# A matrix product with leaky ReLU: 32-bit transposes of A, and a first unit of k in two half segments

## Chip, cores, metric

One core of a Trainium2 chip. The metric is the device time of one execution in microseconds (us); quoted times are medians of repeated executions. "Spell" below means a stretch in which TensorE runs at half clock: in the trace its weight loads then follow each other every 427 ns and not every 216. In the kernel before, the granted clock is 0.50 from 102.5 to 109.3 us, where such a stretch lies. At the start only the pitch of 427 ns tells: the record of the granted clock begins only at 13.75 us in the trace of before. "Full clock" means the pitch of 216.

## The reference

```python
def setup_inputs():
    m, k, n = 4096, 4096, 4096
    return {"a": np.random.randn(m, k).astype(np.float32),
            "b": np.random.randn(k, n).astype(np.float32),
            "alpha": np.float32(0.01)}

def reference(a, b, alpha):
    x = np.matmul(a, b)
    return np.where(x > 0, x, alpha * x)
```

## The kernel before

The product is made in bf16, in regions of 512 rows by 1024 columns: 4 x 2 tiles of 128x512, each in one of eight PSUM buffers (`banks` in the code). k is cut into units of 1024, that is 8 groups of 128. A comes to SBUF with k along the free axis and is transposed there. In the steady part a piece of A (256 rows, one unit) is fetched by four GpSimd DMAs, which also round it to bf16 (128 KB each as written), and transposed by VectorE; the code lays it out in blocks of 32x32 for this:

```python
KC, NT, MT, NP = 8, 512, 4, 2
TURNS = [[0], [1], [2, 3]]

def new_a(mb, h, u):                    # A transposed, one unit of one half: 512 rows
    at[mb, h, u] = at_pool.tile([P, KC, RM], BF16, name="at")

def load_a(mb, h, u, mp):
    dst = new_a(mb, h, u)[:, :, 2 * mp * P:2 * (mp + 1) * P]
    row = (mb * HALVES + h) * RM + 2 * mp * P
    a16 = a16_pool.tile([P, 8, QW], BF16, name="a16")
    for q in range(4):
        src = a[row:row + 2 * P, u * KW + q * QW:u * KW + (q + 1) * QW]
        nc.gpsimd.dma_start(a16[32 * q:32 * q + 32], src.rearrange("(g i) w -> i g w", i=32))
    nc.vector.transpose(
        dst.rearrange("p c (g i) -> p g c i", g=8), a16.rearrange("p g (j c) -> p g c j", c=KC)
    )

def mm(ps, mb, h, pi, u, mt, nt, c, first, last):
    nc.tensor.matmul(ps, at[mb, h, u][:, c, mt * P:(mt + 1) * P],
                     bt[pi, u][:, c, nt * NT:(nt + 1) * NT], start=first, stop=last)
```

The first two regions (half 0 and half 1 of the first 1024 rows) are computed while the data is still arriving. They share one set of B, and go by "turns" over k: unit 0 for half 0, then for half 1; unit 1 likewise; then units 2 and 3 for half 0, and for half 1. A "step" is one unit for one half. At the end of a turn the banks are emptied ("spilled") into SBUF, and from the second turn on added to what lies there:

```python
# the start: unit 0 of half 0 comes as fp32 by SyncE's DMAs, without GpSimd
order = [("a", 0), ("b", 0), ("a", 1), ("b", 1), ("b", 2), ("a", 2), ("b", 3), ("a", 3),
         ("b", 4), ("b", 5), ("b", 6), ("b", 7)]           # 512 KB each
# ... each is cast to bf16; rows of A are transposed by TensorE against an identity
#     and copied to `at`; what has arrived is multiplied
if (what, i) == ("b", 3):
    nc.gpsimd.tensor_copy(x[:, :1], b0[:, 2, :1])   # marker: GpSimd's loads wait for this

for i in range(1, len(steps)):
    t, h, u, first, last = steps[i]
    following = queue[i + 1] if 2 <= i and i + 1 < len(steps) else []   # the next step's loads
    # ...
    for quarter in range(4):
        # 16 matmuls; in the last step of a turn they finish one row of tiles
        if last:
            spill(t, h, quarter, banks)      # VectorE: two adds
        quarter_of(following, quarter)       # with it the next step's transposes, on VectorE too
```

The order of emission is the order on each engine: with `spill` ahead of `quarter_of`, VectorE adds first and transposes for the next step after that (in the trace two adds from 98.45 us, the transposes behind them from 99.66).

Of the kernel before, what the change touches and what calls it, by code (L numbers as in the profile page):

```python
# [8 lines left out]
P = 128  # L9
BF16 = mybir.dt.bfloat16  # L10
FP32 = mybir.dt.float32
LRELU = mybir.ActivationFunctionType.Lrelu
KC = 8
NT = 512
MT = 4
NP = 2
# [3 lines left out]
TURNS = [[0], [1], [2, 3]]  # L20
# [3 lines left out]
def kernel(  # L24
# [17 lines left out]

    nc = tc.nc
    M, K = a.shape
# [3 lines left out]

    KW = KC * P
    KU = K // KW  # L50
    RM = MT * P
    RN = NP * NT
    QW = KW // 4
    HALVES = 2
    MB = M // (HALVES * RM)
    NB = N // RN
    assert TURNS[0] == [0] and sorted(sum(TURNS, [])) == list(range(KU))
# [27 lines left out]
    def new_a(mb, h, u):  # L85
        if (mb, h, u) not in at:
            at[mb, h, u] = at_pool.tile([P, KC, RM], BF16, name="at")
        return at[mb, h, u]
# [6 lines left out]
    def load_a(mb, h, u, mp):  # L95

        dst = new_a(mb, h, u)[:, :, 2 * mp * P:2 * (mp + 1) * P]
        row = (mb * HALVES + h) * RM + 2 * mp * P
        a16 = a16_pool.tile([P, 8, QW], BF16, name="a16")
        for q in range(4):  # L100
            src = a[row:row + 2 * P, u * KW + q * QW:u * KW + (q + 1) * QW]
            nc.gpsimd.dma_start(a16[32 * q:32 * q + 32], src.rearrange("(g i) w -> i g w", i=32))  # L102
        nc.vector.transpose(  # L103
            dst.rearrange("p c (g i) -> p g c i", g=8), a16.rearrange("p g (j c) -> p g c j", c=KC)
        )

    def b_rows(n, u, c):
        src = b[u * KW:(u + 1) * KW, n * RN:(n + 1) * RN]
        return src.rearrange("(p c) n -> p c n", c=KC)[:, c, :]

    def load_b(pi, n, u, c):

        nc.gpsimd.dma_start(new_b(pi, u)[:, c, :], b_rows(n, u, c))  # L113

    def mm(ps, mb, h, pi, u, mt, nt, c, first, last):
        nc.tensor.matmul(  # L116
            ps,
            at[mb, h, u][:, c, mt * P:(mt + 1) * P],
            bt[pi, u][:, c, nt * NT:(nt + 1) * NT],
            start=first,  # L120
            stop=last,
        )
# [24 lines left out]
    for pi in range(1, len(pairs)):  # L147
        first = next(i for i, r in enumerate(regions) if r[2] == pi)
        for u in range(KU):
            lead = 2 if pi == 1 else KU  # L150
            loads.setdefault(first * KU + u - lead, []).extend(
                lambda pi=pi, u=u, c=c: load_b(pi, pairs[pi], u, c) for c in range(KC)
            )
    for mb in range(1, MB):
        first = next(i for i, r in enumerate(regions) if r[0] == mb)
        for h in range(HALVES):
            for u in range(KU):
                loads.setdefault(first * KU + h * KU + u - 2 * KU + 1, []).extend(
                    lambda mb=mb, h=h, u=u, mp=mp: load_a(mb, h, u, mp) for mp in range(MT // 2)
                )  # L160

    def quarter_of(pieces, quarter):
# [5 lines left out]
        (t, h, u, i == 0, i == len(turn) - 1)  # L168
        for t, turn in enumerate(TURNS)
        for h in range(HALVES)  # L170
        for i, u in enumerate(turn)
    ]

    def step_loads(h, u):
        if h:
            return [lambda mp=mp: load_a(0, 1, u, mp) for mp in range(MT // 2)]
        made = [lambda c=c: load_b(0, pairs[0], u, c) for c in range(KC)]
        made.insert(4, lambda: load_a(0, 0, u, 1))
        made.insert(0, lambda: load_a(0, 0, u, 0))
        return made  # L180

    queue = [step_loads(h, u) for _, h, u, _, _ in steps]
    part = {}

    def spill(t, h, mt, banks):
# [10 lines left out]
        if t == len(TURNS) - 1:  # L196
# [4 lines left out]

    a_in = bt_pool.tile([P, MT, KW], FP32, name="a_in", tag="bt")
    b_in = [part_pool.tile([P, KC // 2, RN], FP32, name="b_in", tag="part") for _ in range(2)]
    a_rounded = at_pool.tile([P, MT, KW], BF16, name="a_rounded", tag="at")
    order = [("a", 0), ("b", 0), ("a", 1), ("b", 1), ("b", 2), ("a", 2), ("b", 3), ("a", 3),
             ("b", 4), ("b", 5), ("b", 6), ("b", 7)]
    for what, i in order:
        if what == "a":
            nc.sync.dma_start(a_in[:, i, :], a[i * P:(i + 1) * P, :KW])  # L209
        else:  # L210
            nc.sync.dma_start(b_in[i // 4][:, i % 4, :], b_rows(pairs[0], 0, i))  # L211
    a0 = new_a(0, 0, 0)
    b0 = new_b(0, 0)
    turned = {
        (mt, i): psum_pool.tile([P, KC // 2, P], BF16, name="turned", tag="ps")
        for mt in range(MT)
        for i in range(2)
    }
    banks = new_banks()

    def take(what, i):
        if what == "b":
            nc.scalar.copy(b0[:, i, :], b_in[i // 4][:, i % 4, :])  # L223
            return
        nc.vector.tensor_copy(a_rounded[:, i, :], a_in[:, i, :])  # L225
        cols = a_rounded[:, i, :].rearrange("m (p c) -> m c p", c=KC)
        for c in range(KC):
            nc.tensor.transpose(turned[i, c // 4][:, c % 4, :], cols[:, c, :], ident)  # L228
        nc.scalar.copy(a0[:, :4, i * P:(i + 1) * P], turned[i, 0])  # L229
        nc.vector.tensor_copy(a0[:, 4:, i * P:(i + 1) * P], turned[i, 1])  # L230
# [4 lines left out]
    for n, (what, i) in enumerate(order):  # L235
        take(what, i)
        if (what, i) == ("b", 3):

            nc.gpsimd.tensor_copy(x[:, :1], b0[:, 2, :1])  # L239
        there[what].append(i)  # L240
        now = [(i, c) for c in there["b"]] if what == "a" else [(mt, i) for mt in there["a"]]
        ready.append(now)
        for mt, c in ready[n - 1] if n else []:
            for nt in range(NP):
                mm(banks[mt, nt], 0, 0, 0, 0, mt, nt, c, (mt, nt) not in begun, False)
                begun.add((mt, nt))
    for piece in queue[1]:
        piece()
    part[0] = part_pool.tile([P, MT, RN], FP32, name="part", tag="part")
    for mt, c in ready[-1]:  # L250
        for nt in range(NP):
            mm(banks[mt, nt], 0, 0, 0, 0, mt, nt, c, False, True)
        spill(0, 0, mt, banks)
    for piece in queue[2]:
        piece()

    for i in range(1, len(steps)):
        t, h, u, first, last = steps[i]
# [6 lines left out]
        for quarter in range(4):  # L265
            if last:
                todo = [(quarter, c) for c in range(KC)]
            else:
                todo = [(mt, c) for c in (2 * quarter, 2 * quarter + 1) for mt in range(MT)]
            for mt, c in todo:  # L270
                for nt in range(NP):
                    mm(banks[mt, nt], 0, h, 0, u, mt, nt, c, first and c == 0,
                       last and c == KC - 1)
            if last:
                spill(t, h, quarter, banks)
            quarter_of(following, quarter)
            if own >= 2 * KU - 2:
                quarter_of(loads.get(own, []), quarter)
# [62 lines left out]
```

## Time and profile before

| | before |
|---|---|
| median of 3 runs | 1795.21 us (1794.66 to 1795.24) |
| profiled run | 1796.25 us, span 1794.5 us |
| 8192 matmuls at the trace's pitch of 215.8 ns | 1767.8 us |
| TensorE busy | 99% |
| VectorE's transposes | 62, 235.6 us |

Two views are added. First the chain that ended last, as shares of the span by engine:

```profile
PE 97%; DMA 2%; issue 1%; DVE 0%; ACT 0%; POOL 0%; SPq 0%; DVEq 0%; POOLq 0%
```

97% of it is matmul; most of the rest lies in the first 104 us. Then VectorE's timeline around the last turn (start, duration, engine, line, operation, out<-in, count, and in brackets the idle time before and what ended it):

```profile
98.45 1.29 DVE L195 TENSOR_TENSOR part<-ps,part 128x512 f32<-128x512 f32 x2 [0.65 <-PE ps L116]
99.66 11.19 DVE L103 STREAM_TRANSPOSE at<-a 128x2048 bf16<-128x2048 bf16 x3
...
133.12 1.29 DVE L195 TENSOR_TENSOR part<-ps,part 128x512 f32<-128x512 f32 x2 [2.17 <-remote]
```

The first two lines are the wait of 4.00 us at 103.50: the transpose that the second half needs stands behind two adds and takes 3.8 us. The last line is the last pair of adds of the first two regions. Its start is the mark for the end of these two regions: from there to the end, the execution takes 1796.25 - 133.12 = 1663.1 us.

### The profile page before, as it was taken

The page shows a single profiled execution, that of the slowest core. Times are in us where ns is not written, and L with a number is a line of the kernel's source. Part 1 is how long each engine was busy: PE and PEld are TensorE (multiplying, and loading weights), DVE is VectorE, ACT ScalarE, POOL GpSimd, SP SyncE. Part 2 cuts the span into 40 slices and gives each one's busy share as a digit, 9 for nine tenths or more (in the row PEclk, how much of TensorE's full clock was granted, in tenths as well). Part 3 has the DMA queues.
Part 4 walks back from the last instruction along what each step waited for, and adds up shares of the span by engine and source line. Part 5 has one row for each costly group of instructions (what it writes and reads, how often), then busy time and mean ns, then how long its engine had stood idle before and what let it go on. Part 6 is the DMA issues. An engine that isn't in the chain of part 4 may idle for free.

```text
span 1794.5 us, 17965 instructions
## 1 busy us (share of the span) xinstructions
PE 1771.5 (99%) x8068; PEld 806.3 (45%) x8232; DVE 264.3 (15%) x112; ACT 155.1 (9%) x270; POOL 360.7 (20%) x663
## 2 busy tenths in 40 slices
PE   8999999999999999999999999999999999999999
PEld 4434444444444444444444444444444444444444
DVE  5750000055300000005520000000551000000000
ACT  3010000000000000000000000000000000000001
POOL 4530110333002021033300202004320120201000
PEclk9999999999999999999999999999999999999999
DMA  9993571987319256298713916539770481835511
GB/s 253 195 239 86 122 160 47 182 127 123 85 58 194 55 118 141 63 200 124 122 56 88 192 48 117 119 94 197 125 124 24 101 180 48 157 78 117 118 47 47
DMA packets 147020, 214.06 MB, mean 119 GB/s; under 512 B 12800, under 2 KB 76288, under 8 KB 146944
## 3 DMA queue, kind: packets, MB, share of 16 engines
q0 software_dynamic: 126208, 139.50, 48.1%
q10 hardware_dynamic: 17856, 65.02, 9.3%
q1 hardware_dynamic: 2880, 8.39, 1.2%
q8 instruction: 64, 1.05, 0.2%
q14 instruction: 12, 0.10, 0.0%
HBM read 285.21 MB, written 67.11 MB: 196 GB/s over the span
## 4 chain that ended last, share of the span: by engine, by line
PE 97%; DMA 2%; issue 1%; DVE 0%; ACT 0%; POOL 0%; SPq 0%; DVEq 0%; POOLq 0%
PE ps L116 97%; DMA a<-in_a_dram 1%; DMA a_in<-in_a_dram 0%; DVE at L103 0%; DVE part L195 0%; PE turned L228 0%; ACT part L193 0%; POOL a L102 0%; DVE a_rounded L225 0%; ACT o L300 0%; SPq L211 0%; SPq L209 0%; DVEq L195 0%; POOLq L102 0%
## 5 line engine op out<-in xcount | busy, mean ns | idle before, releaser
L116 PE MATMUL ps<-bt,at 128*128 128x512 bf16 x8028 | 1765.0, 380 | 14.9 <-DVE at L103 5.5
L116 PEld LDWEIGHTS <-at 128*128 128x128 bf16 x8192 | 802.3, 98 | 976.1 <-DVE at L103 7.4
L113 POOL DMA_DIRECT2D bt<-in_b_dram x408 | 217.3, 539 | 1097.4 <-PE ps L116 908.0
L103 DVE STREAM_TRANSPOSE at<-a 128x2048 bf16<-128x2048 bf16 x62 | 235.6, 3842 | 1046.0 <-PE ps L116 1033.7
L300 ACT ACTIVATE o<-ps 128x512 f32<-128x512 f32 x240 | 130.7, 595 | 1524.6 <-PE ps L116 1462.5
L102 POOL DMA_DIRECT2D a<-in_a_dram x248 | 142.3, 579 | 201.3 <-DVE at L103 142.8
L195 DVE TENSOR_TENSOR part<-ps,part 128x512 f32<-128x512 f32 x32 | 20.3, 680 | 33.7 <-PE ps L116 31.6
L198 ACT ACTIVATE o<-part 128x1024 f32<-128x1024 f32 x8 | 8.5, 1057 | 86.0 <-DVE part L195 79.2
L223 ACT CAST bt<-b_in 128x1024 bf16<-128x1024 f32 x8 | 8.1, 1045 | 2.2 <-DMA b_in<-in_b_dram 2.0
L228 PE MATMUL turned<-ident,a_rounded 128*128 128x128 bf16 x32 | 3.6, 276 | 3.3 <-DVE a_rounded L225 3.3
L193 ACT COPY part<-ps 128x512 f32<-128x512 f32 x8 | 4.4, 594 | 14.2 <-PE ps L116 14.2
L228 PEld LDWEIGHTS <-a_rounded 128*128 128x128 bf16 x32 | 3.1, 156 | 5.2 <-DVE a_rounded L225 4.7
L191 DVE COPY part<-ps 128x512 f32<-128x512 f32 x8 | 5.2, 838 | 0.0
L80 PE MATMUL ps<-w 128*128 128x512 bf16 x8 | 3.6, 631 | 1.2 <-DVE x L76 1.2
L225 DVE CAST a_rounded<-a_in 128x1024 bf16<-128x1024 f32 x4 | 2.8, 693 | 6.5 <-DMA a_in<-in_a_dram 6.5
L229 ACT COPY at<-turned 128x512 bf16<-128x512 bf16 x4 | 2.3, 585 | 8.6 <-PE turned L228 8.6
L239 POOL CAST x<-bt 128x1 f32<-128x1 bf16 x1 | 0.6, 558 | 11.1 <-ACT bt L223 11.1
L230 DVE COPY at<-turned 128x512 bf16<-128x512 bf16 x4 | 1.7, 424 | 5.2 <-PE turned L228 5.2
L80 PEld LDWEIGHTS <-w 128*128 128x128 bf16 x8 | 1.0, 142 | 2.8 <-issue 1.6
L77 ACT ACT_TABLE_LOAD x1 | 1.3, 1283 | 0.7 <-PEq L322 0.7
L74 DVE MEMSET w<- 128x256 uint32 x1 | 0.3, 272 | 0.9 <-PEq L322 0.9
masks.py:199 POOL TENSOR_SCALAR_AFFINE_SELECT ident<-ident 128x128 bf16<-128x128 bf16 x1 | 0.3, 287 | 0.1
(7 smaller groups left out, 0.9 us busy)
## 6 DMA issues: line engine op xcount, KB each, us to landing
bt<-in_b_dram POOLq DMA_DIRECT2D x408, 256.0 KB, 7.6
out_dram<-o ACTq DMA_DIRECT2D x124, 512.0 KB, 3.8
a<-in_a_dram POOLq DMA_DIRECT2D x248, 128.0 KB, 5.0
b_in<-in_b_dram SPq DMA_DIRECT2D x8, 512.0 KB, 9.6
a_in<-in_a_dram SPq DMA_DIRECT2D x4, 512.0 KB, 7.8
out_dram<-o SPq DMA_DIRECT2D x8, 256.0 KB, 2.0
```

Source lines behind the costliest of these rows:

```text
L80: nc.tensor.matmul(wp, w[:, :P], w, start=True, stop=True)
L102: nc.gpsimd.dma_start(a16[32 * q:32 * q + 32], src.rearrange("(g i) w -> i g w", i=32))
L103: nc.vector.transpose(dst.rearrange("p c (g i) -> p g c i", g=8), a16.rearrange("p g (j c) -> p g c j", c=KC))
L113: nc.gpsimd.dma_start(new_b(pi, u)[:, c, :], b_rows(n, u, c))
L116: nc.tensor.matmul(ps, at[mb, h, u][:, c, mt * P:(mt + 1) * P], bt[pi, u][:, c, nt * NT:(nt + 1) * NT], start=first, stop=last,)
L191: nc.vector.tensor_copy(kept, banks[mt, nt])
L193: nc.scalar.copy(kept, banks[mt, nt])
L195: nc.vector.tensor_add(kept, banks[mt, nt], kept)
L198: nc.scalar.activation(o, part[h][:, mt, :], LRELU, alpha=alpha)
L223: nc.scalar.copy(b0[:, i, :], b_in[i // 4][:, i % 4, :])
L228: nc.tensor.transpose(turned[i, c // 4][:, c % 4, :], cols[:, c, :], ident)
L300: nc.scalar.activation(o[:, cols], banks[mt, nt], LRELU, alpha=alpha)
```

## The change

Intent: halve VectorE's time per transpose; have less data to wait for before the first work, and keep TensorE's clock up until it comes. Four parts:

1. Two neighbouring bf16 of k are transposed as one 32-bit word. `at` becomes `[P, KC // 2, RM, 2]`, so a matmul's weights are every second bf16.
2. Unit 0 is split into half segments of 512 in k, each with a turn of its own. The third turn now has three segments.
3. The start fetches 256 KB pieces of A and half as much B; the last row of B comes in two halves.
4. Four more dummy matmuls (their result is not used; they keep TensorE busy) between the first transposes and the first real matmul; the marker waits for B's row 1, not 2.

The diff, cut to its core:

```diff
+SEGS = [(0, 0, 4), (0, 4, 4), (1, 0, 8), (2, 0, 8), (3, 0, 8)]   # unit, first group, groups
-TURNS = [[0], [1], [2, 3]]
+TURNS = [[0], [1], [2, 3, 4]]
-            at[mb, h, u] = at_pool.tile([P, KC, RM], BF16, name="at")
+            at[mb, h, u] = at_pool.tile([P, KC // 2, RM, 2], BF16, name="at")
-    def load_a(mb, h, u, mp):
+    def load_a(mb, h, s, mt, tiles):
+        u, c0, kc = SEGS[s]
+        dst = new_a(mb, h, u)[:, c0 // 2:(c0 + kc) // 2, mt * P:(mt + tiles) * P, :]
+        a16 = a16_pool.tile([P, 4 * tiles, kw // 4], BF16, name="a16")
         nc.vector.transpose(
-            dst.rearrange("p c (g i) -> p g c i", g=8), a16.rearrange("p g (j c) -> p g c j", c=KC)
+            dst.rearrange("p c m e -> p c (m e)").bitcast(U32)
+            .rearrange("p c (g i) -> p g c i", g=4 * tiles),
+            a16.rearrange("p g w -> p (g w)").bitcast(U32)
+            .rearrange("p (g j c) -> p g c j", g=4 * tiles, c=kc // 2),
         )
+    def pieces_a(mb, h, s):
+        tiles = 2 * KC // SEGS[s][2]          # a half segment: all 512 rows in one piece
+        return [lambda mt=mt: load_a(mb, h, s, mt, tiles) for mt in range(0, MT, tiles)]
-            at[mb, h, u][:, c, mt * P:(mt + 1) * P],
+            at[mb, h, u][:, c // 2, mt * P:(mt + 1) * P, c % 2],
 ...
-    order = [("a", 0), ("b", 0), ("a", 1), ("b", 1), ("b", 2), ...]
+    for i in range(MT):
+        order += [("a", i, None)] + [("b", i, half) for half in ((0, 1) if i == MT - 1 else (None,))]
 ...
+        if n == 0:
+            for _ in range(4):
+                nc.tensor.matmul(wp, w[:, :P], w, start=True, stop=True)
-        if (what, i) == ("b", 3):
-            nc.gpsimd.tensor_copy(x[:, :1], b0[:, 2, :1])
+        if (what, i) == ("b", 1):
+            nc.gpsimd.tensor_copy(x[:, :1], b0[:, 1, :1])
```

More of the change, by code (lines that the diff above doesn't have):

```diff
@@ L11 @@
 FP32 = mybir.dt.float32
+U32 = mybir.dt.uint32
 LRELU = mybir.ActivationFunctionType.Lrelu
 KC = 8
+SEGS = [(0, 0, 4), (0, 4, 4), (1, 0, 8), (2, 0, 8), (3, 0, 8)]
 NT = 512
@@ L47 @@
     alpha = float(alpha)
-    KW = KC * P
-    KU = K // KW
+    KU = K // (KC * P)
     RM = MT * P
     RN = NP * NT
-    QW = KW // 4
     HALVES = 2
@@ L56 @@
     NB = N // RN
-    assert TURNS[0] == [0] and sorted(sum(TURNS, [])) == list(range(KU))
+    assert TURNS[0] == [0] and sorted(sum(TURNS, [])) == list(range(len(SEGS)))
+    assert sum(kc for _, _, kc in SEGS) * P == K
+    SEGS_OF = [[s for s in range(len(SEGS)) if SEGS[s][0] == u] for u in range(KU)]
     small_pool = ctx.enter_context(tc.tile_pool(name="small", bufs=1))
@@ L93, in new_b, with k_of, b_rows, load_b @@
         return bt[pi, u]
-    def load_a(mb, h, u, mp):
-        dst = new_a(mb, h, u)[:, :, 2 * mp * P:2 * (mp + 1) * P]
-        row = (mb * HALVES + h) * RM + 2 * mp * P
-        a16 = a16_pool.tile([P, 8, QW], BF16, name="a16")
+    def k_of(s):
+        u, c0, kc = SEGS[s]
+        return (u * KC + c0) * P, kc * P
+    def load_a(mb, h, s, mt, tiles):
+        u, c0, kc = SEGS[s]
+        k0, kw = k_of(s)
+        dst = new_a(mb, h, u)[:, c0 // 2:(c0 + kc) // 2, mt * P:(mt + tiles) * P, :]
+        row = ((mb * HALVES + h) * MT + mt) * P
+        a16 = a16_pool.tile([P, 4 * tiles, kw // 4], BF16, name="a16")
         for q in range(4):
-            src = a[row:row + 2 * P, u * KW + q * QW:u * KW + (q + 1) * QW]
+            src = a[row:row + tiles * P, k0 + q * kw // 4:k0 + (q + 1) * kw // 4]
             nc.gpsimd.dma_start(a16[32 * q:32 * q + 32], src.rearrange("(g i) w -> i g w", i=32))
         nc.vector.transpose(
-            dst.rearrange("p c (g i) -> p g c i", g=8), a16.rearrange("p g (j c) -> p g c j", c=KC)
-        )
-    def b_rows(n, u, c):
-        src = b[u * KW:(u + 1) * KW, n * RN:(n + 1) * RN]
-        return src.rearrange("(p c) n -> p c n", c=KC)[:, c, :]
-    def load_b(pi, n, u, c):
-        nc.gpsimd.dma_start(new_b(pi, u)[:, c, :], b_rows(n, u, c))
+            dst.rearrange("p c m e -> p c (m e)").bitcast(U32)
+            .rearrange("p c (g i) -> p g c i", g=4 * tiles),
+            a16.rearrange("p g w -> p (g w)").bitcast(U32)
+            .rearrange("p (g j c) -> p g c j", g=4 * tiles, c=kc // 2),
+        )
+    def b_rows(n, s, c):
+        k0, kw = k_of(s)
+        src = b[k0:k0 + kw, n * RN:(n + 1) * RN]
+        return src.rearrange("(p c) n -> p c n", p=P)[:, c, :]
+    def load_b(pi, n, s, c):
+        u, c0, _ = SEGS[s]
+        nc.gpsimd.dma_start(new_b(pi, u)[:, c0 + c, :], b_rows(n, s, c))
+    def pieces_a(mb, h, s):
+        tiles = 2 * KC // SEGS[s][2]
+        return [lambda mt=mt: load_a(mb, h, s, mt, tiles) for mt in range(0, MT, tiles)]
+    def pieces_b(pi, s):
+        return [lambda c=c: load_b(pi, pairs[pi], s, c) for c in range(SEGS[s][2])]
     def mm(ps, mb, h, pi, u, mt, nt, c, first, last):
@@ L150 @@
             lead = 2 if pi == 1 else KU
-            loads.setdefault(first * KU + u - lead, []).extend(
-                lambda pi=pi, u=u, c=c: load_b(pi, pairs[pi], u, c) for c in range(KC)
-            )
+            for s in SEGS_OF[u]:
+                loads.setdefault(first * KU + u - lead, []).extend(pieces_b(pi, s))
     for mb in range(1, MB):
@@ L157 @@
             for u in range(KU):
-                loads.setdefault(first * KU + h * KU + u - 2 * KU + 1, []).extend(
-                    lambda mb=mb, h=h, u=u, mp=mp: load_a(mb, h, u, mp) for mp in range(MT // 2)
-                )
+                for s in SEGS_OF[u]:
+                    at_slot = first * KU + h * KU + u - 2 * KU + 1
+                    loads.setdefault(at_slot, []).extend(pieces_a(mb, h, s))
     def quarter_of(pieces, quarter):
@@ L167, with step_loads @@
     steps = [
-        (t, h, u, i == 0, i == len(turn) - 1)
+        (t, h, s, i == 0, i == len(turn) - 1)
         for t, turn in enumerate(TURNS)
         for h in range(HALVES)
-        for i, u in enumerate(turn)
+        for i, s in enumerate(turn)
     ]
-    def step_loads(h, u):
-        if h:
-            return [lambda mp=mp: load_a(0, 1, u, mp) for mp in range(MT // 2)]
-        made = [lambda c=c: load_b(0, pairs[0], u, c) for c in range(KC)]
-        made.insert(4, lambda: load_a(0, 0, u, 1))
-        made.insert(0, lambda: load_a(0, 0, u, 0))
+    def step_loads(h, s):
+        made = pieces_a(0, h, s)
+        if h == 0:
+            own = pieces_b(0, s)
+            made = made[:1] + own[:4] + made[1:] + own[4:]
         return made
-    queue = [step_loads(h, u) for _, h, u, _, _ in steps]
+    queue = [step_loads(h, s) for _, h, s, _, _ in steps]
     part = {}
@@ L199, in spill @@
             nc.scalar.dma_start(place(0, h, pairs[0], mt), o)
-    a_in = bt_pool.tile([P, MT, KW], FP32, name="a_in", tag="bt")
-    b_in = [part_pool.tile([P, KC // 2, RN], FP32, name="b_in", tag="part") for _ in range(2)]
-    a_rounded = at_pool.tile([P, MT, KW], BF16, name="a_rounded", tag="at")
-    order = [("a", 0), ("b", 0), ("a", 1), ("b", 1), ("b", 2), ("a", 2), ("b", 3), ("a", 3),
-             ("b", 4), ("b", 5), ("b", 6), ("b", 7)]
-    for what, i in order:
+    kw0 = k_of(0)[1]
@@ new lines, with columns @@
+    kc0 = SEGS[0][2]
+    a_in = bt_pool.tile([P, MT, kw0], FP32, name="a_in", tag="bt")
+    b_in = part_pool.tile([P, kc0, RN], FP32, name="b_in", tag="part")
+    a_rounded = a16_pool.tile([P, MT, kw0], BF16, name="a_rounded", tag="a16")
+    order = []
+    for i in range(MT):
+        order += [("a", i, None)] + [("b", i, half) for half in ((0, 1) if i == MT - 1 else (None,))]
+    def columns(half):
+        return slice(0, RN) if half is None else slice(half * NT, (half + 1) * NT)
+    for what, i, half in order:
@@ L208 @@
         if what == "a":
-            nc.sync.dma_start(a_in[:, i, :], a[i * P:(i + 1) * P, :KW])
+            nc.sync.dma_start(a_in[:, i, :], a[i * P:(i + 1) * P, :kw0])
         else:
-            nc.sync.dma_start(b_in[i // 4][:, i % 4, :], b_rows(pairs[0], 0, i))
+            nc.sync.dma_start(b_in[:, i, columns(half)], b_rows(pairs[0], 0, i)[:, columns(half)])
     a0 = new_a(0, 0, 0)
     b0 = new_b(0, 0)
-    turned = {
-        (mt, i): psum_pool.tile([P, KC // 2, P], BF16, name="turned", tag="ps")
-        for mt in range(MT)
-        for i in range(2)
-    }
@@ L219, with take @@
-    banks = new_banks()
-    def take(what, i):
+    turned = [psum_pool.tile([P, kc0, P], BF16, name="turned", tag="ps") for _ in range(MT)]
+    def take(what, i, half):
         if what == "b":
-            nc.scalar.copy(b0[:, i, :], b_in[i // 4][:, i % 4, :])
+            copy = nc.vector.tensor_copy if half == 1 else nc.scalar.copy
+            copy(b0[:, i, columns(half)], b_in[:, i, columns(half)])
             return
         nc.vector.tensor_copy(a_rounded[:, i, :], a_in[:, i, :])
-        cols = a_rounded[:, i, :].rearrange("m (p c) -> m c p", c=KC)
-        for c in range(KC):
-            nc.tensor.transpose(turned[i, c // 4][:, c % 4, :], cols[:, c, :], ident)
-        nc.scalar.copy(a0[:, :4, i * P:(i + 1) * P], turned[i, 0])
-        nc.vector.tensor_copy(a0[:, 4:, i * P:(i + 1) * P], turned[i, 1])
+        cols = a_rounded[:, i, :].rearrange("m (p c) -> m c p", c=kc0)
+        for c in range(kc0):
+            nc.tensor.transpose(turned[i][:, c, :], cols[:, c, :], ident)
+        for c, copy in ((0, nc.scalar.copy), (1, nc.vector.tensor_copy)):
+            copy(
+                a0[:, c, i * P:(i + 1) * P, :].rearrange("p m e -> p e m"),
+                turned[i][:, 2 * c:2 * c + 2, :],
+            )
@@ L234 @@
     begun = set()
-    for n, (what, i) in enumerate(order):
-        take(what, i)
-        if (what, i) == ("b", 3):
-            nc.gpsimd.tensor_copy(x[:, :1], b0[:, 2, :1])
-        there[what].append(i)
-        now = [(i, c) for c in there["b"]] if what == "a" else [(mt, i) for mt in there["a"]]
-        ready.append(now)
-        for mt, c in ready[n - 1] if n else []:
-            for nt in range(NP):
-                mm(banks[mt, nt], 0, 0, 0, 0, mt, nt, c, (mt, nt) not in begun, False)
-                begun.add((mt, nt))
-    for piece in queue[1]:
-        piece()
-    part[0] = part_pool.tile([P, MT, RN], FP32, name="part", tag="part")
-    for mt, c in ready[-1]:
-        for nt in range(NP):
-            mm(banks[mt, nt], 0, 0, 0, 0, mt, nt, c, False, True)
+    banks = {}
+    for n, (what, i, half) in enumerate(order):
+        take(what, i, half)
+        if n == 0:
+            for _ in range(4):
+                nc.tensor.matmul(wp, w[:, :P], w, start=True, stop=True)
+            banks = new_banks()
+        if (what, i) == ("b", 1):
+            nc.gpsimd.tensor_copy(x[:, :1], b0[:, 1, :1])
+            part[0] = part_pool.tile([P, MT, RN], FP32, name="part", tag="part")
+        if half != 1:
+            there[what].append(i)
+        if what == "a":
+            now = [(i, c, nt) for c in there["b"] for nt in range(NP)]
+        else:
+            now = [(mt, i, nt) for mt in there["a"] for nt in (range(NP) if half is None else (half,))]
+        ready.append(now)
+        for mt, c, nt in ready[n - 1] if n else []:
+            mm(banks[mt, nt], 0, 0, 0, 0, mt, nt, c, (mt, nt) not in begun,
+               what == "b" and half == 1 and c == kc0 - 1)
+            begun.add((mt, nt))
+    following = list(queue[1])
+    following.pop(0)()
+    for mt, c, nt in ready[-1]:
+        mm(banks[mt, nt], 0, 0, 0, 0, mt, nt, c, False, True)
         spill(0, 0, mt, banks)
-    for piece in queue[2]:
+    for piece in following + queue[2]:
         piece()
     for i in range(1, len(steps)):
-        t, h, u, first, last = steps[i]
+        t, h, s, first, last = steps[i]
+        u, c0, kc = SEGS[s]
         following = queue[i + 1] if 2 <= i and i + 1 < len(steps) else []
@@ L266 @@
             if last:
-                todo = [(quarter, c) for c in range(KC)]
+                todo = [(quarter, c) for c in range(kc)]
             else:
-                todo = [(mt, c) for c in (2 * quarter, 2 * quarter + 1) for mt in range(MT)]
+                todo = [(mt, quarter * kc // 4 + c) for c in range(kc // 4) for mt in range(MT)]
             for mt, c in todo:
                 for nt in range(NP):
-                    mm(banks[mt, nt], 0, h, 0, u, mt, nt, c, first and c == 0,
-                       last and c == KC - 1)
+                    mm(banks[mt, nt], 0, h, 0, u, mt, nt, c0 + c, first and c == 0,
+                       last and c == kc - 1)
             if last:
```

## The prediction

> **What bounds the kernel now.** First the page's busy table and the group of the matmuls:
>
> ```profile
> PE 1771.5 (99%) x8068; PEld 806.3 (45%) x8232; DVE 264.3 (15%) x112; ACT 155.1 (9%) x270; POOL 360.7 (20%) x663
> ...
> L116 PE MATMUL ps<-bt,at 128*128 128x512 bf16 x8028 | 1765.0, 380 | 14.9 <-DVE at L103 5.5
> L116 PEld LDWEIGHTS <-at 128*128 128x128 bf16 x8192 | 802.3, 98 | 976.1 <-DVE at L103 7.4
> L103 DVE STREAM_TRANSPOSE at<-a 128x2048 bf16<-128x2048 bf16 x62 | 235.6, 3842 | 1046.0 <-PE ps L116 1033.7
> ```
>
> TensorE is full. The shape asks for 32 x 32 x 8 = 8192 matmuls of 128x512; the trace holds 8192 weight loads and 8028 matmuls, so about 1 matmul record in 50 is missing. The chain of waits gives the pitch:
>
> ```profile
> 198.31 10.74 PE ps L116 x49
> 209.10 10.74 PE ps L116 x49
> 219.90 10.74 PE ps L116 x49
> ```
>
> A piece lasts 10.79 us and holds 49 records, hence 50 matmuls: 215.8 ns each. 8192 x 0.2158 = 1767.8 us. The profiled span is 1794.5, so only 26.7 us (1.5%) is not matmul at full pace, and nothing that keeps all 8192 matmuls at this pace can win 2%.
>
> The timeline of the start and of the first 135 us says where the 26.7 us are:
>
> ```profile
> 4.33 0.69 DVE L225 CAST a_rounded<-a_in 128x1024 bf16<-128x1024 f32 x1 [3.18 <-DMA a_in<-in_a_dram]
> 8.38 0.69 DVE L225 CAST a_rounded<-a_in 128x1024 bf16<-128x1024 f32 x1 [1.77 <-DMA a_in<-in_a_dram]
> 10.00 3.62 PE L116 MATMUL ps<-bt,at 128*128 128x512 bf16 x8
> 13.42 0.65 PEld L228 LDWEIGHTS <-a_rounded 128*128 128x128 bf16 x7 [0.26 <-issue]
> 27.39 17.87 PE L116 MATMUL ps<-bt,at 128*128 128x512 bf16 x81 [0.60 <-ACT part L193]
> 71.40 0.73 PE L116 MATMUL ps<-bt,at 128*128 128x512 bf16 x2 [1.54 <-DVE at L103]
> 72.35 27.14 PE L116 MATMUL ps<-bt,at 128*128 128x512 bf16 x123 [0.22 <-DVE part L195]
> 103.50 56.78 PE L116 MATMUL ps<-bt,at 128*128 128x512 bf16 x244 [4.00 <-DVE at L103]
> 108.59 0.15 PEld L116 LDWEIGHTS <-at 128*128 128x128 bf16 x1 [0.28 <-issue]
> 109.02 0.15 PEld L116 LDWEIGHTS <-at 128*128 128x128 bf16 x1 [0.27 <-issue]
> ```
>
> The first real matmul starts at 10.0 us. The next eight run 427 ns apart (half clock): 8 x 0.21 = 1.7. Two later batches of transposes of A on TensorE, 0.66 each: 1.3. Waits of 0.6, 1.8 (1.54 + 0.22) and 4.0, and behind the last one 14 matmuls again 427 ns apart: 3.0. The last matmul ends at 1790.9: a tail of 3.6. Sum 10.0 + 1.7 + 1.3 + 0.6 + 1.8 + 4.0 + 3.0 + 3.6 = 26.0 of 26.7. So 22.4 us are lost in the first two regions (to about 133 us), and only these can change.
>
> [...] The new layout makes every weight load read each second bf16. The trace has strided loads already: the transposes' loads step by 8 elements and take, warm, 0.65/7 = 93 ns, against 98 ns for the dense ones; both lie under a 216 ns matmul. [...] The trace: 1.54 us of waiting left the clock alone, 4.0 us halved it, for 6 us. [...] The trace shows 3842/2048 = 1.88 ns per 16-bit element; it has no 32-bit transpose.
>
> **The change, part by part.**
>
> *32-bit transposes.* A piece of 2048 bf16 becomes 1024 words. At 1.88 ns per element that is 1.9 us in place of 3.84; I take 1.3 to 2.0 us. 62 become 63, so VectorE drops by some 120 us of 235. It isn't the bound; this counts only where TensorE waits for a transpose: the 1.8 and the 4.0 above. The matmul's pace I leave at 215.8.
>
> *The start.* A pieces fall from 512 to 256 KB (k is halved), B pieces stay 512, the last B is cut in two: 3.15 MB before the first step is complete, not 6.3. In the trace the first bytes move at 1.7 us, 0.73 MB by 4 us, 2.12 by 8, 3.73 by 12, and a piece is usable 1.1 to 1.9 us after its last byte. Then A0 is usable at 3.6, B0 at 5.7, A1 at 6.5, B1 8.1, A2 8.8, B2 10.2, A3 10.9, last B 12.2. A cast of 512 takes about 0.42. Eight dummies run to 4.6, A0's four transposes to 5.2, four dummies to 6.9, A1's transposes to 7.3: without a gap, so the first real matmul comes at 7.3, at full clock (saves 2.7 of the 10.0 and the 1.7). Then data paces it: A2's transposes at 9.3 (1.1 us idle), A3's at 11.4, the last matmul of this step at about 16.1. Its 32 matmuls are 6.9 us of work: 9.2 lost, against 13.0 for the 64 before. **Gain 3.8.**
>
> *What the half segments add.* Step 1 (the other half of A's rows) needs one transpose of 512 rows. Its four DMAs are issued after the marker, when B1 is cast (9.2 + 0.6): from 9.9, 0.6 each as on the page. Landing is some 7 us after the first issue (1.8 of issue plus the 5.0 median, with twice as many, shorter packets): 17 to 18; transposed by 19.3 where TensorE was free at 16.1. **Loss about 3.2** (0.6 before). The built program lets 8 GpSimd DMAs be in flight, so the B of the next segment leaves only when these have landed: **0.5** more for step 2. Step 3 is the sure one: its only A piece is transposed, by VectorE's order, behind the last two adds of step 2. After that step's last matmul come 1.2 us of adds and 1.3 to 2.0 of transpose: **3.0** of wait, new. (Before, the step had two pieces, the first transposed in mid-step: no wait at 55 us.) Step 4 waits for its second transpose and for the banks that the adds behind it free: about **1.4** (1.8 before). The last turn is now three segments long and takes all of B before the second half: 27 MB by about 80 us at 0.37 to 0.4 MB/us is just in time: **1.0**, for its third segment. The second half's first step, which waited 4.0, waits 1.2 + 2.0 for its second piece, less four matmuls (0.9): **2.4**, and the 3.0 at half clock should go.
>
> *Sum.* After: 9.2 + 3.2 + 0.5 + 3.0 + 1.4 + 1.0 + 2.4 = 20.7, against 22.4. [...] I give each 1 in 4 for another 3 us: 1.5. That leaves 22.2: nothing won on average; without a cold spell 1793.5. As the smaller of my transpose times would take about 2 us off three waits, I settle at 1793.
>
> **Rivals.** (a) *The waits of the half segments are hidden, and the start counts in full*: transposes of 1.2 us, DMAs landing by 16.5. The lost time falls to about 16: 1788. For it: less than half as much data ahead of step 1. Against it: the fixed order of adds and transpose in step 3. (b) *Transfers become the bound*: the A pieces of a half segment write runs of 256 B, not 512, 8 in flight; in the trace the DMA share stays above 1 up to 150 us, so there is little slack. Each of the seven steps could slip by 1 us, and two waits go cold: 1803 to 1808. (c) *Strided weights slow every pair*: each nanosecond per matmul is 8.2 us; 4.5 ns would make it 2% slower. Against it: 93 ns at a step of 8 elements.
>
> **Range and chances.** The gain at the start (3.8) and at the second half's first step (4.6) are set against new waits of like size (2.6 + 0.5 + 3.0 + 1.0). The optimistic ends give 1788, a single cold spell 1797, two 1800. 8 in 10: 1786 to 1801. Faster by 2% needs under 1759.3, below the 1767.8 of pure matmuls: 0.01. Slower by 2% needs rival (c) or much of (b): 0.02. Same: 0.97.
>
> **What would show it.** First real matmul near 7.3 us and at 216 ns pitch; first step over near 16; waits of about 3 us ahead of steps 1 and 3 (near 16 and 33 us), the latter on a transpose that starts behind adds; 2.4 in place of 4.0 near 85 us with no loads at 427 ns; 32-bit transposes of 1.3 to 2.0 us; still 50 matmuls per 10.79 us; the same 3.6 of tail. A pitch off 215.8 by over 1 ns would wreck it, and so would cold spells in more than two places.

The sum stands at 9.2 + 3.2 + 0.5 + 3.0 + 1.4 + 1.0 + 2.4 = 20.7, with 1.5 for spells 22.2, against 22.4 before. "Each 1 in 4" is of the two waits of about 3 us, ahead of steps 1 and 3; this chance is the author's estimate, the trace having shown only that the clock was down after a wait of 4.0 us (granted 0.50) and not after one of 1.54. That a 32-bit word costs as much as a 16-bit element (1.88 ns, hence 1.9 us) was the author's assumption, and the lower end of 1.3 us an estimate; no trace showed a 32-bit transpose then. The 1.1 to 1.9 us from a piece's last byte to its use are an estimate too: counted packet by packet, the twelve pieces land 0.7 to 1.9 us after their bytes are in. The 0.37 to 0.4 MB/us are fp32 bytes read, twice the bf16 bytes written, of which the trace of before has 0.19 to 0.21 MB/us in stretches of 4 us from 28 to 80 us.

## The result, and the profile after

| | before | after |
|---|---|---|
| median, runs of the same rounds | 1794.93 us (1793.51 to 1795.24) | 1792.86 us (1791.90 to 1793.81) |
| ratio of the means, 95% interval | | 0.999 (0.9973 to 1.0007) |
| profiled run; span | 1796.25; 1794.5 us | 1792.31; 1790.5 us |
| start of the last adds | 133.12 us | 128.99 us |
| VectorE busy | 264.3 us | 141.9 us |

A ratio here is the mean time of one kernel's runs over that of the other's of the same rounds, so it is not quite the ratio of the medians quoted. Its interval includes 1, here and in the repeat (e11): neither alone tells the gain of 2 us from none, though both have the same sign and the trace is shorter by 4.0. The two profiled runs differ by 3.9 us, the medians by 2.1: the profiled run of before was slower than any of its timed ones, and the runs of after scatter by 1.9 us. A spell of 8 matmuls costs 8 x 0.21 = 1.7 us, and in the runs of after at 1793.4 and 1793.8 us the mean clock was 0.999 and 0.998, against 1.000 in the two faster ones.

The page of after, busy times and the groups that answer to those of before (busy, mean ns | idle before, and what ended most of it):

```profile
PE 1775.6 (99%) x8220; PEld 803.6 (45%) x8220; DVE 141.9 (8%) x114; ACT 150.1 (8%) x266; POOL 369.0 (21%) x671
...
L139 PEld LDWEIGHTS <-at 128*128 128x128 bf16 x8192 | 801.0, 98 | 976.7 <-DVE at L114 10.0
L114 DVE STREAM_TRANSPOSE at<-a 128x1024 uint32<-128x1024 uint32 x63 | 113.0, 1828 | 1165.9 <-DMA a<-in_a_dram 607.8
```

A weight load takes 98 ns as before, though it now reads every second bf16; both traces hold 927 weight loads in 200 us of the steady part, 215.7 ns each. The transposes fell from 235.6 us to 113.0.

The start and the first two regions, TensorE's timeline of after:

```profile
6.97 1.31 PE L139 MATMUL ps<-bt,at 128*128 128x512 bf16 x4
...
10.88 4.48 PE L139 MATMUL ps<-bt,at 128*128 128x512 bf16 x20
17.43 13.99 PE L139 MATMUL ps<-bt,at 128*128 128x512 bf16 x64 [2.07 <-DVE at L114]
33.81 7.95 PE L139 MATMUL ps<-bt,at 128*128 128x512 bf16 x36 [2.39 <-DVE at L114]
43.15 0.94 PE L139 MATMUL ps<-bt,at 128*128 128x512 bf16 x3 [1.40 <-DVE at L114]
44.31 29.30 PE L139 MATMUL ps<-bt,at 128*128 128x512 bf16 x135 [0.22 <-DVE part L216]
74.40 11.81 PE L139 MATMUL ps<-bt,at 128*128 128x512 bf16 x54 [0.79 <-DMA bt<-in_b_dram]
88.42 61.90 PE L139 MATMUL ps<-bt,at 128*128 128x512 bf16 x286 [2.20 <-DVE at L114]
```

The first real matmul comes 3 us earlier, at full clock, and the wait of 4.00 is 2.20. In exchange TensorE waits ahead of step 1 (17.43), step 3 (33.81), step 4 (43.15) and the third segment (74.40), where before it waited 0.60 and 1.76. VectorE's timeline shows what step 3 waits for:

```profile
31.31 1.29 DVE L216 TENSOR_TENSOR part<-ps,part 128x512 f32<-128x512 f32 x2 [0.44 <-PE ps L139]
32.52 1.23 DVE L114 STREAM_TRANSPOSE at<-a 128x1024 uint32<-128x1024 uint32 x1
...
36.81 2.02 DVE L114 STREAM_TRANSPOSE at<-a 128x1024 uint32<-128x1024 uint32 x1
```

The one piece of A that the step needs is transposed behind the last two adds of the step before. The piece of a half segment takes 1.23 us, that of a whole one 2.02, with as many words in it. In the code, VectorE reads a whole piece in steps of 4 words (16 bytes) and a half segment's in steps of 2 (8 bytes). In e2 the same two reads of 2048 bf16 took 3.82 and 2.30 us. The shape of the pieces differs as well, but in e7, where a half segment's piece has 256 rows as a whole piece has, its 512 words took 0.69 to 0.71 us at a step of 8 bytes.

Last the chain of waits. For the whole execution it has 95% TensorE and 4% DMA, where before it had 97% and 2%. Three of its pieces:

```profile
17.30 8.35 DMA a<-in_a_dram
...
28.33 6.85 DMA bt<-in_b_dram
...
66.91 7.45 DMA bt<-in_b_dram
```

From the marker (8.63 us) to 74.40 us the chain is almost only transfers. GpSimd's DMAs wait for one another (the traces of before and after have up to 8 of them in flight, never more), and at a steady 184 to 213 GB/s written from 16 us on (stretches of 4 us), the last row of B for the third turn lands at 74.36 us. TensorE's waits at 17, 33 and 43 us lie beside that.

### The profile page after: what moved, and what is told of

Same layout as the page of the kernel before. It is cut to its first block, busy times and chain, and to the rows that moved or that the text cites. A ratio compares the mean times of both kernels' runs of the same rounds, so it can differ in the third digit from the quotient of the medians. Undisturbed runs are those within 1.5% of the kernel's fastest.

```text
span 1790.5 us, 18113 instructions
## 1 busy us (share of the span) xinstructions
PE 1775.6 (99%) x8220; PEld 803.6 (45%) x8220; DVE 141.9 (8%) x114; ACT 150.1 (8%) x266; POOL 369.0 (21%) x671
## 3 DMA queue, kind: packets, MB, share of 16 engines
q8 instruction: 64, 1.05, 0.2%
## 4 chain that ended last, share of the span: by engine, by line
PE 95%; DMA 4%; POOL 0%; issue 0%; DVE 0%; ACT 0%; SPq 0%; DVEq 0%
PE ps L139 95%; DMA bt<-in_b_dram 2%; DMA a<-in_a_dram 1%; DMA a_in<-in_a_dram 0%; POOL a L113 0%; DVE at L114 0%; POOL bt L129 0%; ACT bt L247 0%; DVE part L216 0%; ACT o L336 0%; ACT at L254 0%; DVE a_rounded L249 0%; PE turned L252 0%; SPq L239 0%; SPq L237 0%
## 5 line engine op out<-in xcount | busy, mean ns | idle before, releaser
L114 DVE STREAM_TRANSPOSE at<-a 128x1024 uint32<-128x1024 uint32 x63 | 113.0, 1828 | 1165.9 <-DMA a<-in_a_dram 607.8
L113 POOL DMA_DIRECT2D a<-in_a_dram x252 | 148.5, 596 | 190.4 <-DVE at L114 125.4
L247 ACT CAST bt<-b_in 128x1024 bf16<-128x1024 f32 (+1 forms) x4 | 3.8, 938 | 0.0
```

What stands on the lines that cost most here:

```text
L114: nc.vector.transpose(dst.rearrange("p c m e -> p c (m e)").bitcast(U32) .rearrange("p c (g i) -> p g c i", g=4 * tiles), a16.rearrange("p ...
L247: copy(b0[:, i, columns(half)], b_in[:, i, columns(half)])
```

## The experiments

Twelve kernels ran (e11 is the changed kernel again), all correct. Time, ratio to before, and the start of the last adds in the profiled run:

| label | us (range) | ratio (95%) | last adds |
|---|---|---|---|
| e1_bits_only | 1788.22 (1787.40 to 1790.74) | 0.9967 (0.9954 to 0.9979) | 126.43 |
| e2_sixteen_bits | 1805.22 (1803.30 to 1806.44) | 1.0058 (1.0045 to 1.0072) | 141.27 |
| e3_no_extra_dummies | 1794.07 (1791.94 to 1794.88) | 0.9995 (0.9983 to 1.0008) | 128.61 |
| e4_early_transposes | 1790.72 (1789.07 to 1790.87) | 0.9975 (0.9962 to 0.9987) | 127.36 |
| e5_more_turns | 1790.98 (1788.71 to 1792.61) | 0.9979 (0.9965 to 0.9992) | 125.39 |
| e6_turns_early | 1786.35 (1785.78 to 1788.02) | 0.9953 (0.9940 to 0.9965) | 122.74 |
| e7_two_pieces | 1793.26 (1791.75 to 1793.51) | 0.9987 (0.9975 to 1.0000) | 129.34 |
| e8_bits_early | 1785.60 (1784.83 to 1786.21) | 0.9946 (0.9934 to 0.9959) | 122.23 |
| e9_marker | 1784.55 (1784.52 to 1784.94) | 0.9945 (0.9933 to 0.9958) | 121.61 |
| e10_dummies | 1785.30 (1784.45 to 1785.74) | 0.9948 (0.9936 to 0.9961) | 121.29 |
| e11_after_again | 1792.44 (1791.30 to 1794.88) | 0.9992 (0.9978 to 1.0006) | 129.09 |
| e12_marker_alone | 1791.92 (1791.02 to 1792.95) | 0.9983 (0.9969 to 0.9996) | 129.63 |

The median of before was 1794.68 to 1795.32. The first four ran on one chip, the next seven on another, e12 on a third.

### One part alone: 32-bit transposes in the kernel before

```diff
 # before +
-tile([P, KC, RM], BF16)
+tile([P, KC // 2, RM, 2], BF16)   # transposes bitcast to U32, weights [:, c // 2, rows, c % 2]
```

> The kernel before with the 32-bit transposes alone; segments, turns and start stay as they were. Theory (the wide transpose is what gains, the split gives nothing on balance): transposes fall from 3.84 to 2.0 us; the wait of 4.0 us at the second half of the last turn becomes 2.2 as in the changed kernel, and with it the half-clock spell (3.0) goes; the wait near 70 us (1.8) goes; the last adds of the first pair of regions start near 126.5 instead of 133.1 us. Time 1788 to 1791, at or below the changed kernel's 1792.9. Rival (start and split carry the gain): 1794 to 1795.

Measured: 1788.22 us, 6.5 below before, and 4.6 below the whole change (4.1 by the two ratios to before). TensorE's timeline, from the fourth batch of A's start to the second half:

```profile
15.82 80.02 PE L120 MATMUL ps<-bt,at 128*128 128x512 bf16 x370
98.06 52.29 PE L120 MATMUL ps<-bt,at 128*128 128x512 bf16 x234 [2.21 <-DVE at L104]
```

80 us without a wait, then 2.21 in place of 4.00; 7 weight loads at half clock follow it, where before had 14. The mark moves by 6.7: 0.7 from a somewhat earlier first matmul (9.33 against 10.00, where TensorE waits for a transfer that the edit doesn't touch, so presumably chance), 0.6 and 1.8 for the two waits that are gone, 1.8 at the second half, 1.5 of half clock: 6.4. So the other parts of the change together cost about 4 us in the presence of this one.

### The other parts without this one: 16-bit transposes in the changed kernel

```diff
 # after, with the layout, transposes and weights of before
-tile([P, KC // 2, RM, 2], BF16)
+tile([P, KC, RM], BF16)
```

> The changed kernel with 16-bit transposes. Theory: transposes of 3.8 us lengthen the waits ahead of steps 1 and 3 from 2.1 and 2.4 to 4.6 and 5.0 us, and the 2.2 of the second half to 4.0; all three are then long enough for half-clock spells of some 3 us. The wait for B at the third segment disappears. Time 1800 to 1810, slower than both kernels. Rival (the start's gain stands whatever the transposes cost): 1791 to 1795.

Measured: 1805.22 us, 10.5 above before. VectorE's and TensorE's timelines:

```profile
34.46 2.30 DVE L114 STREAM_TRANSPOSE at<-a 128x2048 bf16<-128x2048 bf16 x1
41.30 3.82 DVE L114 STREAM_TRANSPOSE at<-a 128x2048 bf16<-128x2048 bf16 x1
```

```profile
36.82 10.65 PE L137 MATMUL ps<-bt,at 128*128 128x512 bf16 x36 [3.46 <-DVE at L114]
...
99.01 51.29 PE L137 MATMUL ps<-bt,at 128*128 128x512 bf16 x229 [4.00 <-DVE at L114]
```

Steps 1, 3, 4 and the second half wait 2.34, 3.46, 3.74 and 4.00 us, and a spell of 7 matmuls or more follows each. The expectation was too high for steps 1 and 3 (4.6 and 5.0): a half segment's transpose takes 2.30 us and not 3.8, also in 16 bits. The split makes the kernel lean on VectorE in four places; in it the 32-bit transposes are worth 12 to 13 us, against 6.5 in the kernel before.

### Without the extra dummies

```diff
-        if n == 0:
-            for _ in range(4):
-                nc.tensor.matmul(wp, w[:, :P], w, start=True, stop=True)
```

> The changed kernel without its four extra dummy matmuls. Theory (up to 74 us the chain of transfers sets the pace, TensorE has slack there): the first matmuls may run at half clock and step 0 ends up to 2 us later, but steps 1 and 6 begin when their data is there: the wait ahead of step 1 shrinks from 2.07, step 6's B still lands near 74.4, the last adds of the two regions start at 129 +- 0.3 us, time within 0.5 us of the changed kernel. Rival (TensorE's own chain): 1 to 2 us slower.

Measured: step 0 ends at 16.81 us instead of 15.36, since a few matmuls run at half clock, but the wait ahead of step 1 is 0.32 instead of 2.07, and the mark is at 128.61 against 128.99. The profiled run, the fastest of its five, therefore shows no cost: what TensorE loses at the start it would have spent waiting for the transfer. The median lies 1.2 to 1.6 us above the two of after. They were run at other times. The ranges overlap. Whether the dummies are worth a microsecond is not settled.

### Transposes ahead of the adds

```diff
-            if last:
-                spill(t, h, quarter, banks)
-            quarter_of(following, quarter)
+            if not last or quarter < 3:
+                quarter_of(following, quarter)
+            if last and quarter == 2:
+                quarter_of(following, 3)
+            if last:
+                spill(t, h, quarter, banks)
```

> The changed kernel with each next step's transposes emitted ahead of the adds of quarter 2, instead of behind those of quarter 3. Theory (transfers set the pace up to 74 us): the waits of 2.4 ahead of step 3 and most of the 1.6 ahead of step 4 go, but the wait for B within the third segment grows from 0.8 to 4 or 5 us, as it lands near 74 us as before (a half-clock spell behind it may cost up to 3); only the 2.2 us ahead of the second half is a gain: last adds near 127, time 1790 to 1791.5. Rival (waits of TensorE add up): 5 to 6 us faster, 1787.

Measured: the waits ahead of step 3 (2.39) and the second half (2.20) are gone, 4.6 us together, but the time falls by some 2 only. Step 4 now waits 1.16 and three times 0.22, for banks, and TensorE's timeline near 72 us reads:

```profile
71.03 0.59 PE L139 MATMUL ps<-bt,at 128*128 128x512 bf16 x2 [0.68 <-DMA bt<-in_b_dram]
...
73.67 76.53 PE L139 MATMUL ps<-bt,at 128*128 128x512 bf16 x347 [0.78 <-DMA bt<-in_b_dram]
```

Row after row of B is waited for (0.68, 0.67, 0.78), the last one landing at 73.63 us where it did at 74.36 before; about 7 matmuls at half clock follow. The time was foreseen, the split of it was not: the wait for B was 2.1 us plus a spell, not 4 to 5, because step 4 kept waiting. The result is the point: **2.39 us taken off ahead of the transfers' deadline bought at most 0.7.** Even that may be chance: the first row of B that GpSimd fetches had landed 0.84 us earlier than in after (19.65 against 20.49 us), before any step that the edit changes.

### A turn for segment 2, so that B is wanted later

```diff
-TURNS = [[0], [1], [2, 3, 4]]
+TURNS = [[0], [1], [2], [3, 4]]
```

> The changed kernel with four turns, the last of two segments ([3, 4]), as the kernel before had. Theory (three segments in the last turn pull all of B ahead of the second half's A, so that TensorE waits for B at 73.6 us): that wait of 0.8 goes, step 4 finishes its rows one after the other and so does not wait for its second transpose (1.6 goes); the waits of 2.1, 2.4 and 2.2 stay. Last adds near 126.5 (129.0 in the changed kernel), time 1789.5 to 1791. Rival (transfers are short whatever the order): a wait of the same size turns up elsewhere, time as the changed kernel, 1792 to 1794.

Measured: no wait for B, none ahead of step 4; 1.39, 2.39 and 2.21 remain. The mark moves by 3.6 us, the median by 1.5 to 1.9; the profiled run was the fastest of the five and has no spell.

### Both

```diff
 # after + the edits of e4 and of e5
```

> Both: four turns, and the transposes emitted ahead of the adds of quarter 2. Theory: the waits of 2.4 and 2.2 go as well; but the third segment's first quarter needs all eight rows of B, of which the last lands near 43 us, and TensorE gets there by 41: about 2 us of wait for B come back there. Last adds near 123.5 to 124, time 1786.5 to 1788. Rival (waits add up): 121.5, time 1785. Rival (nothing over the early transposes alone): 1790.5.

Measured: 1786.35 us. One wait is left, 2.05 us ahead of step 1, and this one was followed by 8 weight loads at half clock (18.0 to 21.0 us). The expected wait of 2 us for B did not come: the spell had put TensorE 1.5 us back, and B was there in time. The two edits together take 6.1 to 6.5 us off after, where each alone took about 2, with a scatter of 2 to 4 us in each. The traces say the same: from the start of step 1 to the mark, with the spells taken out (1.4 us in e4, 1.5 in e6), e4 is 2.6 us shorter than after, e5 3.0, and both together 7.6. They remove two things that hide each other.

### Half segments in two pieces as well

```diff
 # the kernel of the last section +
-        tiles = 2 * KC // SEGS[s][2]
+        tiles = 2
```

> As the last one, with the half segments' A in two pieces of 256 rows. Theory: the wait ahead of step 1 (2.07) shrinks by 0.6 to 1.0, as its first half can be transposed while the second lands; but the same bytes have to come before the third segment's B, and the wait for that grows by as much: time within 0.7 us of the one-piece version. Rival: 1 us faster.

Measured: 1793.26 us, 7 slower than e6; both theories are wrong. Step 1's wait is gone, but rows of B come late (0.61, 0.64, 0.64, then 3.11 us with a spell). Stretches of 4 us, with busy time and count of each engine, then clock, DMA share and GB/s; first this kernel, then after:

```profile
24.00:28.00 4.00, 2.81 (x11) 1.07 (x11) 0.68 (x2) 0.00 (x0) 2.62 (x6) 1.00 1.24 125
28.00:32.00 4.00, 3.17 (x15) 1.46 (x15) 4.00 (x8) 0.00 (x0) 4.00 (x8) 1.00 1.19 121
```

```profile
24.00:28.00 4.00, 4.00 (x20) 1.78 (x19) 2.12 (x4) 0.58 (x1) 2.15 (x4) 1.00 1.66 184
28.00:32.00 4.00, 3.42 (x16) 1.37 (x14) 3.12 (x6) 0.00 (x0) 3.23 (x7) 1.00 1.20 209
```

The fifth pair is GpSimd. At 64 KB a DMA costs it nearly as much as at 128: 12 issues took 7.14 us, in after 8 took 5.25, that is 0.60 and 0.66 each (in e7 the medians from issue to landing are 3.9 and 5.1 us). While it issues the small ones, 121 to 125 GB/s arrive and not 184 to 209; B slips, and TensorE waits. The issues alone do not explain it: in the second stretch GpSimd issues without a pause, but in the first it is busy for 2.62 of 4.00 us and otherwise waits for earlier transfers to land. A small DMA also counts as one of the DMAs in flight, of which before and after have 8 at most. Which of the two costs more was not tested.

### No split at all: 32-bit transposes and early emission on the old start

```diff
 # e1 + the edit of e4
```

> The kernel before with 32-bit transposes and the early emission, without the split or the new start. Theory: the one wait left there after the start, 2.2 at the second half of the last turn, goes; last adds near 124.2 (126.4 without), time 1785.5 to 1787.5, below the changed kernel by 6. Rival (transfers are late there too): 1788.

Measured: 1785.60 us, no wait at all after the start. This says what the split is worth: with the same two improvements the kernel with the split and four turns (e6) takes 1786.35.

### The marker on B's first row

```diff
 # e6 +
-        if (what, i) == ("b", 1):
-            nc.gpsimd.tensor_copy(x[:, :1], b0[:, 1, :1])
+        if (what, i) == ("b", 0):
+            nc.gpsimd.tensor_copy(x[:, :1], b0[:, 0, :1])
```

> The version with four turns and early transposes, with the GpSimd marker moved from the second row of B to the first, so that the loads of the other half's A go out some 1.9 us earlier (6.7 instead of 8.6). Theory (the wait ahead of step 1 is the landing of those loads): it shrinks from 2.05 to between 0.3 and 1.2 us, the first step ends up to 0.5 us later as its own pieces share the transfers, and half-clock spells behind it become rarer. Last adds near 120.5 to 121.5 (122.7, of which 1.7 a half-clock spell), time 1784 to 1786. Rival (the bytes in the way are the same): no change, 1786.3.

Measured: 1784.55 us, the best of all, 10.1 below before, with a scatter of only 0.4 us: no spell is left to come and go. TensorE's timeline:

```profile
16.43 23.48 PE L139 MATMUL ps<-bt,at 128*128 128x512 bf16 x106 [1.09 <-DVE at L114]
...
41.77 3.40 PE L139 MATMUL ps<-bt,at 128*128 128x512 bf16 x15 [1.10 <-DMA bt<-in_b_dram]
```

Step 1 waits 1.09 instead of 2.05; a wait of 1.10 (and 0.17) for B appears at 41 us, since TensorE has caught up with the transfers.

### Six dummies on the old start

```diff
 # e8 +
+        if n == 0:
+            for _ in range(6):
+                nc.tensor.matmul(banks[0, 0], w[:, :P], w, start=True, stop=True)
```

> The kernel before with 32-bit transposes and early emission, plus six dummy matmuls between the first and the second block of transposes of A, where TensorE idles from 6.0 to 8.4 us. Theory (there TensorE's own chain bounds the start, unlike in the changed kernel): the first eight real matmuls run at 216 instead of 427 ns, but the third block of A still lands when it does, near 12.4, so of the 1.7 us only what is not waited for there is kept: last adds 0.5 to 1.5 us earlier than 122.2, time 1784 to 1785.5. Rival (no slack used at all): 1785.6.

Measured: the first real matmuls run at full clock, and the mark is 0.9 us earlier than in e8; the median, 1785.30, is 0.3 lower, inside the scatter. So the old start with dummies comes within 0.75 us of the best version of the split.

### The changed kernel again

> The changed kernel unaltered, as a control for the runs of other chips: 1792 to 1794, and in its profile either a half-clock spell of about 8 matmuls behind one of the waits of 2 us (last adds near 130.7) or none (129.0).

Measured, without any edit: 1792.44 us, waits of 2.00, 2.39, 1.39 + 0.22, 0.85 and 2.20, no spell in the profiled run. The result of the change is repeated, beside e9 and e10 on the same chip.

### The marker alone

```diff
 # after + the edit of e9
```

> The changed kernel with the GpSimd marker on the first row of B instead of the second, nothing else. Theory (from the marker to 74.4 us the chain is transfers, one behind the other at a full rate): the first loads go out 1.9 us earlier and land 0.8 us earlier, as they did in the version above, and the B that TensorE waits for at the third segment lands earlier by the same 0.8 to 1.9 us although the waits ahead of steps 3 and 4 stay 2.4 and 1.6: TensorE then arrives there earlier too, since its wait ahead of step 1 shrinks by 0.9. Last adds 128.0 to 128.3 instead of 129.0, time 1791 to 1792. Rival (the rate of transfers after 20 us decides, not their start): last adds 129.0, the wait for B grows to 1.7.

Measured: 1791.92 us, 0.5 to 0.9 below after. Step 1 waits 0.95, step 4 0.57 + 0.22, and no row of B is waited for. In the profiled run the waits of 2.39 and 2.19 were followed by spells of 8 and 7 matmuls; less the second (1.5 us), the mark would be near 128.1, a gain of 0.9. The times do not settle it: the intervals of the two ratios overlap.

## Why the prediction was right or wrong

The time was foreseen to 0.1 us (1793.0; 1792.86 measured), and most steps to within about a microsecond. The first is in part luck: a loss of 20.7 us without spells was foreseen, where the trace has 17.5 to 18.3, and the profiled runs are 4.0 us apart. The medians are only 2.1 apart, since the profiled run of before, from which the prediction took its terms, was 1.3 us slower than the median of before, and that of after, without a spell, 0.5 faster than the median of after. TensorE's loss in the first two regions, by the prediction's terms:

| term, us | before | predicted | measured after |
|---|---|---|---|
| start and step 0 | 13.0 | 9.2 | 8.4 |
| step 1 | 0.6 | 3.2 | 2.07 |
| step 2 | 0 | 0.5 | 0 |
| step 3 | 0 | 3.0 | 2.39 |
| step 4 | 1.8 | 1.4 | 1.62 |
| third segment | 0 | 1.0 | 0.79 |
| second half | 4.0 | 2.4 | 2.20 |
| half clock behind waits | 3.0 | 1.5 | 0 in this run |
| sum | 22.4 | 22.2 | 17.5 |

The sums differ by 4.9 and the spans by 4.0. Counted by the starts of the weight loads, 512 up to the mark, the loss is 22.5 us before and 18.3 after, 4.1 apart: the terms of before come out right, those of after miss 0.8. An idle time is counted from the end of a matmul's record, which lasts 379 ns, while the next matmul would have started after 216. So each stop costs 0.16 us more than the idle time shown, and five of after's six stops leave this out.

- **Pitch, weights, tail: right.** 215.7 ns in both; strided weights cost nothing that shows (rival c is out).
- **Step 0: nearly right.** First real matmul at 6.97 (7.3), step over at 15.36 (16.1).
- **Step 1: a third too large.** The marker ended at 8.82 us, about 1 us earlier than assumed, and the half segment's transpose took 1.24 us.
- **Step 3: right in mechanism.** The transpose stood behind the adds as foreseen. The 3.0 was 1.2 of adds and, in effect, 1.8 of transpose; the transpose took 1.23.
- **32-bit transposes: nearly right** (1.3 to 2.0 predicted; 1.24 and 2.00). That the two kinds of piece would lie at the two ends was not seen.
- **Rivals (a) and (b): each in part.** The lost time came nearer to (a)'s 16 us than to 22.2. Transfers did set the pace up to 74.40 us, as (b) has it, but TensorE waited for B there only 0.79 us, and not 1 us in each of seven steps.
- **Half clock: too rare.** Each wait of 3 us had been given 1 in 4. In the profiled runs, after the start, waits of 2.0 to 2.4 us were followed by a spell in 5 of 15 cases, and those of 3.1 us and more in 5 of 5 (one in before, three in e2, one in e7). Single waits of up to 1.7 us never were; three of 0.7 within 3 us were (e4). A spell behind 2.0 to 2.4 us lasted 7 or 8 matmuls (1.5 to 1.7 us), that behind 4.0 us 14 in before and 8 in e2.
- **What it did not see: the worth of each part.** The prediction's "9.2 + 3.2 + 0.5 + 3.0 + 1.4 + 1.0 + 2.4" accounts for one kernel, and as that it held; it does not say what taking one wait away is worth. The chain shows transfers from 8.6 to 74.4 us, and e4 shows that 2.39 us removed inside that stretch came back as waits for B. The prediction also set "Gain 3.8" for the start against the new waits as the main account. e1 shows a larger one: the 32-bit transposes alone bring 6.5 us, and the other parts take about 4 of them back. What faster transposes are worth without the other parts was never worked out.

So the gain went, in this order: into a wait for A ahead of step 1 (its data is fetched only after the marker), into adds ahead of the transpose at step 3 and the second half, and into the third turn, which with three segments wants all of B by 74 us. Remove the order (e4) and the deadline (e5) together, and 6 us appear (e6); issue A's loads earlier, and 2 more (e9). What the split start then brings over the old start is 0.75 to 1.05 us (e9 against e10 and e8), which is inside the intervals of the ratios; the old start with an earlier marker of its own was not tried. Step 0's loss did fall by 4.6 us, but little of it is left at the end.

Open: the cost of the extra dummies (e3), the worth of the marker alone (e12), and what in e7 holds the transfers back.

## What to carry to other kernels

Before adding up waits of the busiest engine, follow the chain and ask up to which moment transfers set the pace: a wait that lies ahead of their deadline is worth little until the deadline moves (here 2.39 us of it bought at most 0.7). When a change bundles parts, predict each alone in the old kernel too; here one part alone did three times what the whole did. In a loop that empties banks and prepares the next step on one engine, emit the preparation first: that edit of a few lines was worth 2.6 us on top of the 32-bit transposes (e8 against e1, on two chips whose times of before differ by 0.3), and with the turns and the marker it gave the best version, 0.55% below before (e9).
